# Attention in a two-layer trunk: the merge of the three patterns in half steps, the mask made first, v's splits and the affine rows in program order, two rows of o in v's buffer

## The chip, the core and the metric

The kernel runs on one core of a Trainium2 chip. The core has five engines with queues of their own: TensorE (PE in the profile, its weight loads PEld), VectorE (DVE), ScalarE (ACT), GpSimd (POOL) and SyncE (SP), which here issues the DMAs. Each engine takes its instructions in the order in which they were queued and waits, where needed, on semaphores. The metric is the device time of one execution in microseconds; lower is better.

## What is computed

The reference is a trunk of two layers over 1024 tokens of width 1024 in fp32. Layer 0 mixes tokens with a chunked gMLP, layer 1 with causal attention; a squared-ReLU MLP follows each. Each of the four sublayers is x <- LayerNorm(ALPHA * x + gate * f(h)), with h = x * (1 + scale) + shift, and shift, scale and gate from a conditioning vector. The part that the change touches is the attention, cut to its core:

```python
def dilated_branch(q, k, v, window, dilation, slopes):   # span = window // dilation = 128
    s = einsum('bnqrhe,bnkrhe->bnrhqk', qb, kb) * (E ** -0.5)   # kb: this block and the one before
    s = where(valid, s - slopes * dilation * diff, NEG)
    m = max(s); p = exp(s - m); l = sum(p)
    return einsum('bnrhqk,bnkrhe->bnqrhe', p / l, vb), m + log(l)

def mixer_b(h, w_qkv, w_out, slopes):
    qkv = (h @ w_qkv).reshape(B, S, N_PAT, 3, B_HEADS, B_HEAD_DIM)
    for g, (window, dilation) in enumerate(((128, 1), (512, 4), (2048, 16))):
        outs[g], lses[g] = dilated_branch(q_g, k_g, v_g, window, dilation, slopes)
    wts = softmax(lses over g)
    return sum_g(wts_g * outs_g) @ w_out
```

There are 16 heads of width 64, and every pattern g has q, k and v of its own.

## The kernel before

**Products in three passes.** TensorE multiplies pairs of fp32r numbers: a tensor is split into hi (a cast) and lo (what the cast lost), and a product is hi*hi + hi*lo + lo*hi. `split` (L100) makes the pair: the cast runs on ACT (L102), the subtraction on DVE (L103). Nearly every tensor goes through it, so these two lines stand for many tiles in the profile.

**Stages.** Mixer A, MLP 0, the values of all heads (`values`, L1123, which writes v to DRAM), attention (`attention`, L1252), its output projection (`OutRows`, L392), MLP 1. Memory for a stage is opened in pools when the stage is traced; a pool's tiles lie where those of the stage before lay, and each tile waits for the old tiles under it to be released. In `values` the pool at the lowest address holds the left forms S2 and S3, 16 KB of each partition apiece, of which S3 is used later; further up come the held weights, the x tiles and S4. In `attention` the pools are opened in the order `ql`, `vec`, `qk`, `qp` from the same address.

**Attention.** 24 groups, one for each of eight pairs of heads and each pattern in the order g = 2, 1, 0. A group takes eight slots, each with two half slots (`slots`, `at`, L1353 to 1358; here "+6.1" is the second half slot of the sixth slot after a group's first). Scores of a head's tile pairs, their softmax, the transposes of the probabilities (with a split into pThi and pTlo) and the products with v are hung into these slots; `project` (L1307), which computes q and k for the groups to come, is a generator that is advanced two matmul groups after each half slot. So TensorE always has projection matmuls between the steps of the softmax. A projection's PSUM bank, one of two, is released when its four pieces are split into q or k (L1340).

**v.** `load_v` (L1368) loads a group's v from DRAM into `v_raw`, of tag `raw` with two buffers, which the raw weights of q and k share, and splits it into `v`, of which there are two buffers.

**The mask.** `near` (L1270) holds distances, made by POOL with an iota and two selects; `far` is its right half, copied by DVE, with one corner filled. Both lie in `qp`. Each head's `bias` is a scaled copy.

**The merge.** After the three groups of a pair, `merge` (L1495) reads the softmax statistics, computes the weights of the patterns, writes them to DRAM and reads them back spread over the partitions (`bc`, 128x1024, three buffers of tag `res`). Then `scale(g)` multiplies each pattern's output by its weights, for g = 1 and 2 in a permuted order of elements, and `add` sums them; the sum goes to `o_dram`. These five steps on DVE stand in five half slots of the next pair's first group: +5.0, +5.1, +6.0, +6.1, +7.0.

**The affine rows.** `affine_row` (L1569): eight rows of the residual are loaded, multiplied and shifted by POOL and stored, for use after attention. They are hung into every second slot from +2.1 of the first group on, and use `res` buffers.

**The output projection.** `prepare(ch)` splits two rows of o at a time: rows 0 to 3 are loaded into `res` buffers, rows 4 to 6 into the `raw` buffers, the last row stays in SBUF. `out.load` loads the weights through `raw` too.

**The order of the work.** The program text gives a priority, not an order. A planner walks through the traced instructions with estimated durations, and at each point it queues on an engine the instruction that is ready by its estimates and comes first in the program. So an instruction whose inputs are early floats ahead of its place in the text. `tc.keep_in_program_order(ins)` ties an instruction behind the instruction traced just before it on the same engine; what is not tied may still float. The queues are fixed when the kernel is built.

## Time and profile before

| | |
|---|---|
| median of 3 runs | 2797.5 us (2794.14 to 2802.86) |
| profiled execution | 2792.79 us, of which the span from first to last instruction 2791.1 us |
| mean granted TensorE clock | 0.987 |
| busy: PE / DVE / ACT / POOL | 2697.5 / 2036.5 / 1424.1 / 189.2 us |
| attention, first score to last group's first score | 1267.0 to 2035.2 us |
| one pair of heads | 94.2 us (the first), 99.4 to 102.7 us (the next six) |

In a row of the timeline stand the start and the duration in us, the engine, the line, the operation, its tiles (out<-in), shapes and count, and in brackets how long the engine had been idle before it and what ended that. In a row of waits stand who waited, for what, the total in us, the number of times and the longest. In a row of a stretch stand its bounds and length, the busy time and number of instructions of each engine, the granted clock as a share of the full one, the DMA share and GB/s. A group's row has busy us and mean ns of one, then the engine's idle time just before.

### The profile page before, as it was taken

Reading aid. Unit: us, or ns where it says so; the run is one execution under the profiler, and the core shown is the slowest. Engines: PE = TensorE matmul, PEld = TensorE weight load, DVE = VectorE, ACT = ScalarE, POOL = GpSimd, SP = SyncE. Lnnn points to the kernel's source line nnn. Section 1 sums busy time; section 2 is a strip of 40 time slices with the busy share of each in tenths; the row PEclk is TensorE's granted clock in tenths of the full one; section 3 lists DMA queues with packets and bytes.
Section 4 is the critical chain, followed back from the end, with each engine's and each line's share of the span. In section 5 each row is a group of like instructions: output and inputs, shape, how many; then the busy total and the mean of one; then the engine's idle time right before and its main releaser. Section 6 shows DMA issues by size and latency. Waiting matters only on the chain.

```text
span 2791.1 us, 36348 instructions
## 1 busy us (share of the span) xinstructions
PE 2697.5 (97%) x12954; PEld 2244.4 (80%) x12954; DVE 2036.5 (73%) x3600; ACT 1424.1 (51%) x2639; POOL 189.2 (7%) x147
## 2 busy tenths in 40 slices
PE   6999999999999999989999999999998999999998
PEld 5787878887888888878888888888876788878887
DVE  6777797777967795445767767767679975668887
ACT  3354375555443553325665666666563755554332
POOL 1001000000000000043111111111020000000000
PEclk9999999999999999999999999999999999999999
DMA  7533347667845545353222213222234564486562
GB/s 257 166 121 107 120 158 226 219 223 273 295 142 191 165 144 158 121 187 101 62 62 78 74 51 85 77 55 78 85 89 154 171 209 154 158 284 210 171 200 90
DMA packets 317690, 416.63 MB, mean 149 GB/s; under 512 B 49164, under 2 KB 174516, under 8 KB 317508
## 3 DMA queue, kind: packets, MB, share of 16 engines
q1 hardware_dynamic: 317508, 414.31, 46.4%
q8 instruction: 101, 1.65, 0.3%
q14 instruction: 81, 0.66, 0.1%
HBM read 317.69 MB, written 96.55 MB: 148 GB/s over the span
## 4 chain that ended last, share of the span: by engine, by line
PE 73%; DVE 14%; DMA 7%; ACT 3%; issue 2%; POOL 1%; SPq 1%; POOLq 0%; DVEq 0%; ACTq 0%
PE psd L949 21%; PE psua L790 8%; PE psq L1332 8%; PE psk L1332 7%; PE psv L1237 7%; PE psuc L790 4%; PE psd_wout L367 3%; DMA adaw<-in_ada_w_dram 3%; PE pv L1459 2%; PE psu L367 2%; PE psd_wo L367 2%; PE psub L790 2%; PE psv L464 1%; DMA bc<-w_dram 1%; PE sc L1404 1%
## 5 line engine op out<-in xcount | busy, mean ns | idle before, releaser
L790 PE MATMUL psua<-right,left 128*128 128x512 f32 x1536 | 366.2, 392 | 3.3 <-ACT right L102 1.7
L949 PE MATMUL psd<-rhi,lhi 128*128 128x512 f32 x896 | 350.5, 391 | 3.0 <-ACT part L821 3.0
L949 PE MATMUL psd<-rlo,lhi 128*128 128x512 f32 x896 | 350.4, 391 | 0.2
L949 PE MATMUL psd<-rhi,llo 128*128 128x512 f32 x896 | 349.8, 390 | 0.0
L790 PEld LDWEIGHTS psua<-right,left 128*128 128x128 f32 x1536 | 288.1, 189 | 65.5 <-DVE right L103 2.9
L1413 ACT ACTIVATE p<-p,stat 128x128 f32<-128x128 f32 (+1 forms) x384 | 171.2, 446 | 147.2 <-DVE stat L1411 142.4
L949 PEld LDWEIGHTS psd<-rhi,lhi 128*128 128x128 f32 x896 | 168.9, 189 | 39.6 <-ACT part L821 3.9
L949 PEld LDWEIGHTS psd<-rlo,lhi 128*128 128x128 f32 x896 | 168.9, 188 | 36.1 <-DVE rlo L103 1.1
L949 PEld LDWEIGHTS psd<-rhi,llo 128*128 128x128 f32 x896 | 169.0, 189 | 35.1
L1332 PE MATMUL psk<-form_L,wk_hi 128*128 128x512 f32 x576 | 186.9, 406 | 9.7 <-DVE qlo L103 9.7
L790 PE MATMUL psuc<-right,left 128*128 128x512 f32 x768 | 187.8, 391 | 0.0
L1332 PE MATMUL psq<-form_L,wq_hi 128*128 128x512 f32 x576 | 184.9, 402 | 0.0
L103 DVE TENSOR_TENSOR pTlo<-pT,pThi 128x512 fp32r<-128x512 f32 (+1 forms) x160 | 99.6, 623 | 108.8 <-ACT pThi L102 108.5
L128 DVE SCALAR_TENSOR_TENSOR adaacc<-adaw,silu_c,adaacc 128x512 f32<-128x512 f32 x168 | 132.4, 799 | 56.0 <-DMA adaw<-in_ada_w_dram 55.1
L790 PEld LDWEIGHTS psuc<-right,left 128*128 128x128 f32 x768 | 143.4, 188 | 30.0 <-DVE right L103 0.5
L103 DVE TENSOR_TENSOR left<-ws,left 128x512 fp32r<-128x512 f32 x128 | 87.9, 688 | 73.0 <-ACT left L102 71.3
L103 DVE TENSOR_TENSOR llo<-lraw,lhi 128x1024 fp32r<-128x1024 f32 x112 | 136.3, 1217 | 0.8 <-ACT lhi L102 0.8
L102 ACT CAST left<-ws 128x512 fp32r<-128x512 f32 x128 | 79.3, 620 | 96.2 <-DVE ws L711 85.5
L1411 DVE CUSTOM_DVE_ANT_0 p<-sc,bias 128x128 f32<-128x128 f32 (+1 forms) x384 | 122.0, 346 | 8.7 <-PE sc L1405 6.2
L102 ACT CAST rhi<-rraw 128x1024 fp32r<-128x1024 f32 x48 | 50.6, 1054 | 142.9 <-issue 113.7
L1332 PEld LDWEIGHTS psk<-form_L,wk_hi 128*128 128x128 f32 x576 | 101.0, 191 | 25.2 <-issue 10.1
L1237 PE MATMUL psv<-vrhi,form_S 128*128 128x512 f32 x384 | 119.4, 389 | 0.2 <-DVE vpart L1214 0.2
(286 smaller groups left out, 6325.8 us busy)
## 6 DMA issues: line engine op xcount, KB each, us to landing
lraw<-forms SPq DMA_DIRECT2D x112, 512.0 KB
adaw<-in_ada_w_dram SPq DMA_DIRECT2D x192, 256.0 KB
up<-in_mlp_w_up_dram SPq DMA_DIRECT2D x64, 512.0 KB
forms<-s SPq DMA_DIRECT2D x128, 256.0 KB
rraw<-in_mlp_w_down_dram SPq DMA_DIRECT2D x64, 512.0 KB
forms<-part SPq DMA_DIRECT2D x96, 256.0 KB
vraw<-in_b_w_qkv_dram SPq DMA_DIRECT2D x26, 512.0 KB
spill<-acc SPq DMA_DIRECT2D x24, 512.0 KB
```

The source lines that it names most:

```text
L102: first = A.copy(hi, src) if hi_engine is A else hi_engine.tensor_copy(hi, src)
L103: return first, lo_engine.tensor_tensor(lo, src, hi, op=ALU.subtract)
L128: ins = V.scalar_tensor_tensor(acc[:], raw[:], silu_c[:, k : k + 1], acc[:], ALU.mult, ALU.add)
L367: T.matmul(dst, s[a], m[b], start=(n == 0), stop=(n == last))
L464: T.matmul(sums[u, half][:], units[u][a_][:, k * P : (k + 1) * P], hT[half][b_][:, k, :], start=k == 0 and a_ + b_ == 0, stop=k == KD - 1 ...
L790: T.matmul(acc, w[:, a, k, :], right[p][:, b, k, :], start=p in (1, 2, 5) and k + a + b == 0, stop=k == 3 and a == 1, skip_group_check=True)
L949: ins = T.matmul(sums[kind, m][:], l[a][:, k, m * P : (m + 1) * P], r[b][:, k, :], start=p in (1, 5, 2, 3) and kp + k + a + b == 0, stop=k ...
L1237: T.matmul(acc, left[:, a, 2 * kp + k, m * P : (m + 1) * P], r[b][:, k, :], start=p in (1, 2, 5) and kp + k + a + b == 0, stop=kp == 1 and ...
L1332: T.matmul(p[:], wu[a][:, k * P : (k + 1) * P], h_op(k, half, b), start=k + c_ == 0, stop=k == KD - 1 and c_ == 2)
L1411: V.tensor_tensor_reduce(out=pr[:, 0:w], in0=scb[:, sl], in1=st["bias"][:, width - w :], scale=-0.125, scalar=3e38, op0=ALU.add, op1=ALU.m ...
L1413: A.activation(pr[:, 0:w], pr[:, 0:w], AF.Exp, bias=nm, scale=-1.0, accum_out=l)
L1459: T.matmul(pvs[b][:, q0 % HALF : q0 % HALF + w_], stt, x_[:, o_ : o_ + w_], start=not begun[b], stop=left[b] == 0, skip_group_check=True)
```

## The change

It has five parts. `near` and `far` are made in the pool `ql`, ahead of the `qlo` tiles and their fills, which moves 1.5 KB of each partition from the last pool to the first. `load_v` moves from half slot +1 of slot base - 4 to half slot 0, and its split becomes a step of its own, `split_v`, in half slot +1 of slot base - 3, with both instructions tied in program order. `scale` and `add` work on one half of their tile at a time, ten steps in place of five; for the first seven pairs they stand in ten half slots, +6.0 to +10.1, for the last pair in the half slots of before, two each. The two POOL instructions of each affine row are tied in program order. Rows 4 and 5 of o are loaded by one DMA into one tile of v's tag, at the end of `output()`, in place of two `raw` tiles in `prepare(2)`.

```diff
-            near = qp.tile([P, 2 * P], F32, name="near", bufs=1)
+            near = ql.tile([P, 2 * P], F32, name="near")
...
-            far = qp.tile([P, P], F32, name="far", bufs=1)
+            far = ql.tile([P, P], F32, name="far")
             V.tensor_copy(far[:], near[:, P:])
             V.memset(far[64:P, 0:64], FAR)
+            qlo = [[ql.tile([P, S], F32R, name=f"qlo{e}_{b}") for b in range(2)] for e in range(2)]
...
-                @at(max(base - 4, 0), 1)
+                @at(max(base - 4, 0), 0)
                 def load_v():
-                    raw = wts.tile([P, NT, P], F32, name=f"v_raw_{hp}_{g}", tag="raw", bufs=2)
+                    my["raw"] = raw = wts.tile([P, NT, P], F32, name=f"v_raw_{hp}_{g}", tag="raw", bufs=2)
...
+                @at(max(base - 3, 0), 1)
+                def split_v():
+
                     my["v"] = vs = qp.tile([P, NT, 4, HEAD], F32R, name=f"v_{hp}_{g}", tag="v")
-                    split(vs[:, :, 0:4:3, :], vs[:, :, 1:3, :], raw[:].rearrange("p t (e c) -> p t e c", e=2))
+                    for x_ in split(vs[:, :, 0:4:3, :], vs[:, :, 1:3, :], my["raw"][:].rearrange("p t (e c) -> p t e c", e=2)):
+                        tc.keep_in_program_order(x_)
...
-                def scale(g):
+                def scale(g, half):
...
+                    n = o.shape[1] // 2
+                    o, bc = (t[:, half * n : (half + 1) * n] for t in (o, bc))
                     V.tensor_tensor(bc, o, bc, op=ALU.mult)
 
-                def add(g):
-                    V.tensor_tensor(box[0][:], box[0][:], box[g][:], op=ALU.add)
-                    if g == 2:
+                def add(g, half):
+                    w = slice(half * HALF, (half + 1) * HALF)
+                    V.tensor_tensor(box[0][:, w], box[0][:, w], box[g][:, w], op=ALU.add)
+                    if g == 2 and half:
...
-                for n, f in enumerate((lambda: scale(1), lambda: scale(2), lambda: scale(0), lambda: add(1), lambda: add(2))):
-                    at(base + 5 + n // 2, n % 2)(f)
+                steps = [lambda f=f, g=g, half=half: f(g, half) for f, g in ((scale, 1), (scale, 2), (scale, 0), (add, 1), (add, 2)) for half in range(2)]
+                for n, f in enumerate(steps):
+                    n = n + 12 if hp < N_PAIRS - 1 else n // 2 + 10
+                    at(base + n // 2, n % 2)(f)
...
-                G.tensor_tensor(t[:], t[:], affine["g"][:], op=ALU.mult)
-                G.tensor_tensor(t[:], t[:], affine["b"][:], op=ALU.add)
+                for n, op in (("g", ALU.mult), ("b", ALU.add)):
+                    tc.keep_in_program_order(G.tensor_tensor(t[:], t[:], affine[n][:], op=op))
...
+            def load_o(k):
+                if k == 4:
+                    both = qp.tile([P, 2, S], F32, name="oraw_4", tag="v")
+                    nc.sync.dma_start(both[:], o_dram[4:6].rearrange("k p t -> p k t"))
+                    box[5] = both[:, 1, :]
+                    return both[:, 0, :]
+                raw = row_bc(f"oraw_{k}") if k < 4 else wts.tile([P, S], F32, name=f"oraw_{k}", tag="raw", bufs=2)
+                nc.sync.dma_start(raw[:], o_dram[k])
+                return raw[:]
...
-                        raw = row_bc(f"oraw_{k}") if k < 4 else wts.tile([P, S], F32, name=f"oraw_{k}", tag="raw", bufs=2)
-                        nc.sync.dma_start(raw[:], o_dram[k])
+                        raw = box.pop(k, None) or load_o(k)
...
+                box[4] = load_o(4)
                 box["begin"] = out.begin()
```

More of the change, by code (lines that the diff above doesn't have):

```diff
@@ L1590, in prepare @@
                     if k == N_PAIRS - 1:
-                        raw = oTs["sum"]
+                        raw = oTs["sum"][:]
                     else:
-                        raw = row_bc(f"oraw_{k}") if k < 4 else wts.tile([P, S], F32, name=f"oraw_{k}", tag="raw", bufs=2)
-                        nc.sync.dma_start(raw[:], o_dram[k])
+                        raw = box.pop(k, None) or load_o(k)
                     for half in range(2):
```

7 lines of the change are left out of this document (3 added, 4 removed).

## The prediction

> **What bounds the kernel now.** I read the page first, then who waited for whom on TensorE in three stretches, then the stretches by engine, then the timelines of single engines around the long waits.
>
> ```profile
> span 2791.1 us, 36348 instructions
> PE 2697.5 (97%) x12954; PEld 2244.4 (80%) x12954; DVE 2036.5 (73%) x3600; ACT 1424.1 (51%) x2639; POOL 189.2 (7%) x147
> L103 DVE TENSOR_TENSOR left<-ws,left 128x512 fp32r<-128x512 f32 x128 | 87.9, 688 | 73.0 <-ACT left L102 71.3
> L103 DVE TENSOR_TENSOR llo<-lraw,lhi 128x1024 fp32r<-128x1024 f32 x112 | 136.3, 1217 | 0.8 <-ACT lhi L102 0.8
> ```
>
> TensorE is busy in 97% of the span, so only its own waits, and the slow clock behind them, can be won. The waits of 1200 to 1300, 1300 to 2000 and 2000 to 2200 us (total, times, longest) are:
>
> ```profile
> PE psk L1332 <- DVE qlo L103: 9.7, 1, 9.7
> ...
> PE pv L1459 <- DVE pTlo L103: 15.0, 6, 2.5
> ...
> PE psd_wo L367 <- DVE wo_lo L103: 2.4, 1, 2.4
> PE psd_wo L367 <- DVE acc L387: 2.3, 3, 1.0
> PE pv L1459 <- DVE pTlo L103: 2.3, 1, 2.3
> ...
> PE psd_wo L367 <- ACT wo_hi L102: 2.1, 1, 2.1
> ```
>
> So there is one wait of 9.7 us where attention begins, seven of about 2.5 us, one after each of the first seven pairs of heads, and some 7 us around the output projection. The stretches by engine (PE, PEld, DVE, ACT, POOL, then the granted clock) show what a merge costs: six pairs that hold one long wait each, one of these with a lowered clock, one without, and the first pair, which holds no merge.
>
> ```profile
> 1361.20:1967.20 606.00, 589.46 (x3333) 507.17 (x3332) 426.01 (x1074) 380.55 (x973) 69.96 (x72) 0.99 0.26 70
> 1361.20:1462.20 101.00, 98.51 (x558) 84.76 (x557) 71.02 (x179) 63.50 (x163) 11.71 (x12) 0.98 0.26 70
> 1564.90:1664.30 99.40, 96.90 (x557) 83.50 (x556) 70.92 (x179) 63.28 (x163) 11.71 (x12) 1.00 0.27 71
> 1267.00:1361.20 94.20, 94.20 (x535) 81.08 (x533) 59.57 (x156) 61.66 (x158) 24.55 (x18) 1.00 0.26 77
> ```
>
> The pair at full clock takes 99.40 us with 96.90 busy: 96.9 is a pair without a stall.
>
> **The change, part by part.**
>
> *The mask first, the affine rows pinned.* Attention's start on PE, ACT, POOL and DVE:
>
> ```profile
> 1236.88 0.61 PE L1332 MATMUL psq<-form_L,wq_hi 128*128 128x512 f32 x2
> ...
> 1237.56 0.61 PE L1332 MATMUL psq<-form_L,wq_hi 128*128 128x512 f32 x2
> ...
> 1248.10 1.19 PE L1332 MATMUL psk<-form_L,wk_hi 128*128 128x512 f32 x2 [9.70 <-DVE qlo L103]
> ...
> 1253.36 0.66 PE L1332 MATMUL psk<-form_L,wk_hi 128*128 128x512 f32 x2
> ...
> 1233.00 0.58 ACT L102 CAST q<-psq 64x512 fp32r<-64x512 f32 x1 [1.29 <-PE psq L1332]
> 1242.24 1.04 ACT L102 CAST v<-v_raw 128x1024 fp32r<-128x1024 f32 x1 [8.66 <-DMA v_raw<-v]
> ...
> 1241.35 2.35 POOL L1578 TENSOR_TENSOR aff<-aff,aff_b 128x1024 f32<-128x1024 f32 x1
> 1243.64 0.35 POOL L1271 IOTA near<- 128x256 f32 x1
> ...
> 1233.46 1.21 DVE L103 TENSOR_TENSOR wk_lo<-wk_raw,wk_hi 128x1024 fp32r<-128x1024 f32 x1
> 1244.97 0.23 DVE L1277 COPY far<-near 128x128 f32<-128x128 f32 x1 [10.30 <-POOL near L1274]
> 1245.11 0.68 DVE L103 TENSOR_TENSOR qlo<-psq,q 64x512 fp32r<-64x512 f32 x1
> ```
>
> The first projection's bank is released by two casts on ACT, each followed by a subtraction on DVE. The subtraction stands in DVE's queue behind the copy of `far`, which waits for `near`, which POOL makes behind an affine row. A second obstacle is in ACT's queue: the cast of v, waiting for its load, stands between the two casts of q. The change takes away both: the mask lies in the first pool, where S2 lay, and is traced first on POOL; the affine rows and v's split can no longer float ahead of what was traced before them. With both gone, cast, subtraction, cast, subtraction run from 1233.00, with wk_lo (to 1234.67) in between: 1234.67 + 0.68 + 0.58 + 0.68 = 1236.6. TensorE wants the bank after its last warm group, 1237.56 + 2 x 0.39, about 1238.4, so it does not wait. That wins 9.70 us, and the slow clock behind: four groups of three matmuls take 1253.36 - 1248.10 = 5.26 us where a warm group takes 1237.56 - 1236.88 = 0.68, four 2.72, so 2.5 more. Together 12.2 us. If only `far` got out of the way, the cast of v (to 1243.28) would be late next: 1243.28 + 0.58 + 0.68 = 1244.5, a gain of 3.6. I take 12.2, since the code moves both, and keep 3.6 as the lower end. `near` and `far` push the last `qlo` 1.5 KB into S3's place; its fill comes a pair's projections ahead of its use, so I take nothing.
>
> The pinned rows run inside the first pairs now. What a row of POOL does to DVE is seen earlier:
>
> ```profile
> 1205.36 2.39 POOL L1578 TENSOR_TENSOR aff<-aff,aff_b 128x1024 f32<-128x1024 f32 x1
> ...
> 1205.53 3.31 DVE L103 TENSOR_TENSOR vrlo<-v_r,vrhi 128x1024 fp32r<-128x1024 f32 x1 [1.76 <-ACT vrhi L102]
> ...
> 1209.36 1.21 DVE L103 TENSOR_TENSOR vrlo<-v_r,vrhi 128x1024 fp32r<-128x1024 f32 x1
> ```
>
> The same subtraction takes 3.31 us beside POOL and 1.21 alone: 2.1 us lost. In the first three groups stand nine such splits (wq, wk, v), so DVE loses at most 9 x 2.1 = 18.9 us, where it is busy 59.57 of 94.20. I take 0.5 us of TensorE's time, bounds 0 and 18.9. On SP the rows' loads and stores move back along with them, behind each other as before.
>
> *The merge in halves.* Around the fourth pair's merge DVE does this, and TensorE waits behind it:
>
> ```profile
> 1588.77 2.03 DVE L1543 TENSOR_TENSOR bc<-oT,bc 128x1024 f32<-128x1024 f32 x1 [1.02 <-DMA bc<-w_dram]
> 1591.10 2.00 DVE L1543 TENSOR_TENSOR bc<-oT,bc 128x1024 f32<-128x1024 f32 x1 [0.30 <-DMA bc<-w_dram]
> ...
> 1595.50 1.23 DVE L1543 TENSOR_TENSOR bc<-oT,bc 128x1024 f32<-128x1024 f32 x1
> ...
> 1596.97 1.22 DVE L1546 TENSOR_TENSOR bc<-bc,bc 128x1024 f32<-128x1024 f32 x1
> 1598.11 0.68 DVE L103 TENSOR_TENSOR pTlo<-pT,pThi 128x512 fp32r<-128x512 f32 x1
> 1598.71 1.22 DVE L1546 TENSOR_TENSOR bc<-bc,bc 128x1024 f32<-128x1024 f32 x1
> ...
> 1598.85 0.33 PE L1459 MATMUL pv<-pTlo,v 128*128 128x128 f32 x1 [2.50 <-DVE pTlo L103]
> ```
>
> Ahead of pTlo stand four whole steps, 2.03 + 2.00 + 1.23 + 1.22 = 6.48 us, and 1.32 us of waiting for the loads of `bc`. After the change the first half step stands in half slot +6.0, one slot later than now, so that the loads have landed. The pTlo in question belongs to half slot +6.1; two halves are traced before it, and a third may slip in. A half costs 0.688 us against 1.217 whole (the two rows of the page), so 0.16 more per split; the strided ones I estimate at half of 2.0 and 0.08, 1.08. Two or three halves are 2.2 to 3.2 us in place of 6.48 and 1.32: at least 4.6 less, more than the wait of 2.50. It should go.
>
> What is late next are the later packs of probabilities. Ten halves are 4 x 1.08 + 6 x 0.69 = 8.5 us, the five whole ones 7.7. They lie over five slots; eight slots are a third of 99.4, so five are 20.7 us. DVE without a merge is busy 59.57/94.20 = 63%, 13.1 us of these; with the halves 21.6, 0.9 more than there is. So DVE has no time to spare there, and each half that runs late delays a pTlo by up to a microsecond. I take 0.6 us per merge that remains, bounds 0 and the whole 2.5 with its clock.
>
> The seven merges cost now: six pairs 606.0 - 6 x 96.9 = 24.6 us, the seventh its wait of 2.3 and, as the mean of the others, 24.6/6 - 2.5 = 1.6 of slow clock, 3.9; together 28.5. Less 7 x 0.6 = 4.2 that leaves 24.3. The eighth merge keeps its slots; its steps are only cut in two, which lets TensorE's evictions (2.3 us of waits on `acc`) slip in between and costs 0.8 of DVE: nothing.
>
> A rule speaks to the clock part of that sum. The Trainium skill, "TensorE: Matmul & The Clock Gate", section "HAM oscillation", says that the clock falls with idle gaps above about 3.4 us. By it 2.5 us would never lower it, and the seven merges would be worth their waits alone, 15.0 + 2.3 = 17.3 us. The trace differs: 101.00 us at clock 0.98 and 99.40 at 1.00 hold one wait each of the same length (six make 15.0 us, the longest 2.5).
>
> *v's split.* Its load moves half a slot forward, its split to three slots ahead of its group and behind what was traced before it. Now:
>
> ```profile
> 1575.17 0.36 SPq L1373 DMA_DIRECT2D v_raw<-v  x1
> 1579.12 0.37 SPq L352 DMA_DIRECT2D wk_raw<-in_b_w_qkv_dram  x1
> ...
> 1610.00 1.05 ACT L102 CAST v<-v_raw 128x1024 fp32r<-128x1024 f32 x1
> ...
> 1600.26 1.22 DVE L103 TENSOR_TENSOR wk_lo<-wk_raw,wk_hi 128x1024 fp32r<-128x1024 f32 x1
> ```
>
> The load stands 35 us ahead of the split, so ACT doesn't meet an unlanded v. The raw buffer (one of two) stays taken some three slots, 12 us, longer; the loads of weights queued on SP behind it share the other. They stand far ahead too: 21 us for this wk. Nothing, with a loss where that lead is used up.
>
> *Rows of o in v's buffer.* One load of two rows in place of two, after the last but one v is released. SP is past its last projection weights there. Both splits can float, and their use is two partial products away. Nothing; the tail's waits of about 7 us (2.4 + 2.3 + 2.1) are the bound to the good, and to the bad one more such wait, of 2.4 us.
>
> **The sum.** 12.2 + 24.3 - 0.5 = 36.0. The profiled execution took 2792.8 us (span 2791.1 and 1.7 around it): 2756.8. The median of the runs, 2797.5, is 4.7 above; on that footing 2761.
>
> **The rivals.**
>
> *Half of the merge's stall stays* (DVE is full for five slots, and where the order is planned with shorter steps than the 2.0 us of the trace, pTlo comes late again): 12.2 + 14 - 0.5 gives 2772. For it speaks the sum of 21.6 in 20.7 us, against it that pTlo now follows two halves.
>
> *The start's wait passes on* to the cast of v or to another split: 3.6 in place of 12.2, 2770. Against it speaks v's pinned place behind the first scores.
>
> *The affine rows hold DVE up in the first pairs*, each of the nine splits in full: 18.9 on top, 2780. For it speaks the row of 3.31 us; against it the first pair's start, where POOL was as busy (24.55 us in that pair) and TensorE had 94.20 of 94.20. The Trainium skill, "GPSIMD Engine Reference", section "Key points", says that POOL shares its SBUF interfaces with VectorE, with contention where an instruction has two SBUF inputs; the trace agrees, 3.31 beside 1.21.
>
> *Slower: the raw buffers.* v holds one of two longer, projection weights arrive late, TensorE waits for a wq_lo or wk_lo. There are 48 projections; at 36.0/48 = 0.75 us each the gain is gone, and with 1 us each the time is 2809. For it speaks that SP and the buffers are taken in order; against it the lead of 21 us against 12 us of longer holding.
>
> *Nothing moves*: the queues come out as before, 2797.
>
> **How the numbers follow.** My case has 0.62, with 2751 to 2771; half the stall 0.14, the start's wait 0.06, the affine rows 0.05, the raw buffers 0.10, nothing 0.03. Faster by over 0.3% (8 us, about what a measurement of this kernel tells from no change) is 0.87, the same 0.03, slower 0.10. The low end takes the start, all seven merges and the tail: 2797.5 - 12.2 - 28.5 - 7 = 2750; the high end the start alone, 2785.
>
> **What would show it.** POOL makes `near` before 1210 us, DVE has no copy of `far` with a wait in front, and psk follows psq without a gap at full clock. Scores begin about 12 us earlier. Waits of pv on pTlo fall from 2.5 us to under 1 us each, and the pairs take 97 to 98 us at clock 1.00. DVE shows, for each pair, four half steps of about 1.1 us and six of 0.69. Wrong would be: a wait of psq or psk on wq_lo or wk_lo, pTlo still behind several halves, or ACT idle on v_raw.

## The result, and the profile after

The changed kernel takes 2815.7 us (median; 2810.3 to 2821.6) where the kernel before takes 2797.5 (2794.1 to 2802.9): the ratio is 1.0063, with an interval of 1.0040 to 1.0085. So it is 0.6% slower; 2761 had been forecast. The profiled execution of the changed kernel has a span of 2810.4 us, 19.3 more than before. One execution of the experiment e11 below took 8293 us where its other three took 2812 to 2815; its ratio leaves it out. The first two lines of the page of the changed kernel:

```profile
span 2810.4 us, 36355 instructions
PE 2702.6 (96%) x12954; PEld 2246.5 (80%) x12954; DVE 2037.3 (72%) x3640; ACT 1423.1 (51%) x2639; POOL 184.6 (7%) x147
```

The page hardly differs from the one before. The difference shows in the stretches by engine (length, then busy time of PE, PEld, DVE, ACT and POOL, granted clock, DMA). The first row goes from the first projection of the attention to its first score, the second covers the first pair of heads, the third the six pairs that follow, each with one merge in it:

```profile
1227.50:1254.70 27.20, 27.20 (x122) 22.52 (x120) 9.64 (x12) 6.76 (x10) 2.55 (x3) 1.00 0.23 68
1254.70:1373.80 119.10, 101.39 (x534) 85.02 (x533) 65.63 (x159) 63.94 (x161) 51.59 (x28) 0.91 0.37 112
1373.80:1987.10 613.30, 594.61 (x3332) 509.65 (x3331) 428.41 (x1104) 380.86 (x973) 65.08 (x72) 0.98 0.27 69
```

The same stretches of the kernel before, of which only the first was not shown yet:

```profile
1227.40:1267.00 39.60, 29.90 (x121) 24.22 (x120) 15.08 (x17) 10.94 (x14) 20.51 (x14) 0.87 0.63 200
```

The start became 39.6 - 27.2 = 12.4 us shorter, as forecast (12.2). The first pair became 119.1 - 94.2 = 24.9 us longer, and the six pairs 613.3 - 606.0 = 7.3 us longer in place of 21 shorter. What follows them is 0.6 shorter (823.9 before, 823.3 after). Together -12.4 + 24.9 + 7.3 - 0.6 = 19.2, the difference of the spans to a tenth. So two stretches carry the loss.

**The start.** From the timelines of POOL, DVE and PE:

```profile
1195.10 0.35 POOL L1266 IOTA near<- 128x256 f32 x1 [887.53 <-PE psv L1237]
...
1235.08 0.69 DVE L103 TENSOR_TENSOR qlo<-psq,q 64x512 fp32r<-64x512 f32 x1 [0.65 <-ACT q L102]
...
1237.70 0.61 PE L1332 MATMUL psq<-form_L,wq_hi 128*128 128x512 f32 x2
...
1238.38 0.61 PE L1332 MATMUL psk<-form_L,wk_hi 128*128 128x512 f32 x2
```

`near` is made at 1195, the bank's last subtraction ends at 1235.77, and psk follows psq 0.68 us later, without a gap and at full clock.

**The first pair.** TensorE now has one wait of 13.43 us there. Its chain, from the timelines of SP, ACT, DVE and PE:

```profile
1320.28 0.33 SPq L1588 DMA_DIRECT2D spill<-aff  x1
1322.91 0.32 SPq L1585 DMA_DIRECT2D aff<-spill  x1
1331.35 0.32 SPq L1588 DMA_DIRECT2D spill<-aff  x1
1333.93 0.32 SPq L1585 DMA_DIRECT2D aff<-spill  x1
1334.30 0.43 SPq L352 DMA_DIRECT2D wk_raw<-in_b_w_qkv_dram  x1
...
1338.79 1.04 ACT L102 CAST wk_hi<-wk_raw 128x1024 fp32r<-128x1024 f32 x1 [17.34 <-DMA wk_raw<-in_b_w_qkv_dram]
...
1316.66 1.34 DVE L103 TENSOR_TENSOR v<-v_raw,v 128x1024 fp32r<-128x1024 f32 x1 [0.39 <-ACT v L102]
...
1339.86 3.42 DVE L103 TENSOR_TENSOR wk_lo<-wk_raw,wk_hi 128x1024 fp32r<-128x1024 f32 x1 [18.03 <-ACT wk_hi L102]
...
1340.28 0.47 PE L1440 MATMUL pT<-ident,p 128*128 128x128 f32 x1 [13.43 <-ACT p L1417]
```

Read it backwards. TensorE waits for probabilities from ACT. ACT stands 17.34 us at the cast of a raw weight, with the exponentials queued behind it. The weight's load was issued only at 1334.30. v's subtraction, which frees a raw buffer, had ended at 1318.0; the load stands on SP behind stores and loads of affine rows. A row's store waits for POOL; the next load waits for that store, since the rows have one buffer; the next store waits for POOL again. The stores at 1320.28 and 1331.35 are 11.1 us apart, while the program asks for a row every two slots, some 8 us. So the rows fall behind, and what stands behind them on SP falls behind with them. The Trainium skill, "TensorE: Matmul & The Clock Gate", section "Architectural detail: the array is 16× 32×32, not 1× 128×128", says that ACT and DVE take their queues strictly in order; the idle 17.34 and 18.03 us agree.

**The six pairs.** The waits of TensorE in them (total, times, longest) have changed their name, not their size. Before it was 15.0 us on pTlo; after it is

```profile
PE pv L1463 <- ACT pThi L102: 13.2, 6, 2.4
PE pv L1463 <- DVE pTlo L103: 4.3, 6, 0.7
PE pT L1440 <- ACT p L1417: 1.1, 2, 0.6
```

The second merge, on DVE, with the wait on PE behind it:

```profile
1499.63 2.07 DVE L1549 TENSOR_TENSOR bc<-oT,bc 128x512 f32<-128x512 f32 x2 [2.38 <-DMA bc<-w_dram]
1501.62 0.28 DVE L1415 CUSTOM_DVE_ANT_0 p<-sc,bias 128x128 f32<-128x128 f32 x1
...
1502.04 1.03 DVE L1549 TENSOR_TENSOR bc<-oT,bc 128x512 f32<-128x512 f32 x1
1503.85 1.22 DVE L103 TENSOR_TENSOR v<-v_raw,v 128x1024 fp32r<-128x1024 f32 x1 [0.79 <-ACT v L102]
1505.10 0.69 DVE L103 TENSOR_TENSOR k<-psk,k 64x512 fp32r<-64x512 f32 x1
1505.82 1.09 DVE L1549 TENSOR_TENSOR bc<-oT,bc 128x512 f32<-128x512 f32 x1
...
1508.25 0.29 DVE L1415 CUSTOM_DVE_ANT_0 p<-sc,bias 128x128 f32<-128x128 f32 x1
...
1508.68 1.29 DVE L1549 TENSOR_TENSOR bc<-oT,bc 128x512 f32<-128x512 f32 x2
1509.88 0.68 DVE L1553 TENSOR_TENSOR bc<-bc,bc 128x512 f32<-128x512 f32 x1
1510.48 0.68 DVE L103 TENSOR_TENSOR pTlo<-pT,pThi 128x512 fp32r<-128x512 f32 x1
...
1510.18 0.33 PE L1463 MATMUL pv<-pThi,v 128*128 128x128 f32 x1 [2.36 <-ACT pThi L102]
```

Three things stand out. The first half steps wait 2.38 us for `bc`, and the scores of 1501.62 stand behind them; over the six pairs DVE stands 10.2 us in front of the scaled halves, as it did in front of the whole steps before (10.3). v's subtraction stands among the steps and waits 0.79 us for its cast. And seven half steps, not two or three, run ahead of pTlo: they floated forward. Which of the three counts, the trace alone doesn't say.

### The profile page after: what moved, and what is told of

The parts are those of the page before. It is cut to its first block, busy times and chain, and to the rows that moved or that the text cites. A ratio compares the mean times of both kernels' runs of the same rounds, so it can differ in the third digit from the quotient of the medians.

```text
span 2810.4 us, 36355 instructions
## 1 busy us (share of the span) xinstructions
PE 2702.6 (96%) x12954; PEld 2246.5 (80%) x12954; DVE 2037.3 (72%) x3640; ACT 1423.1 (51%) x2639; POOL 184.6 (7%) x147
## 4 chain that ended last, share of the span: by engine, by line
PE 72%; DVE 13%; DMA 8%; ACT 3%; issue 2%; POOL 1%; SPq 0%; POOLq 0%; DVEq 0%; ACTq 0%
PE psd L949 21%; PE psq L1332 8%; PE psv L1237 8%; PE psua L790 7%; PE psk L1332 6%; PE psuc L790 4%; DMA adaw<-in_ada_w_dram 3%; PE psd_wout L367 3%; PE pv L1463 2%; PE psu L367 2%; PE psd_wo L367 2%; PE psub L790 2%; PE psv L464 2%; DVE adaacc L128 1%; PE sc L1408 1%
## 5 line engine op out<-in xcount | busy, mean ns | idle before, releaser
L102 ACT CAST lhi<-lraw 128x1024 fp32r<-128x1024 f32 x112 | 117.3, 1048 | 4.1 <-PE psua L790 2.9
```

Of the source, the lines that this page charges most:

```text
L102: first = A.copy(hi, src) if hi_engine is A else hi_engine.tensor_copy(hi, src)
```

## The experiments

Each kernel is given by its stretches, taken in the same way as above: from the first projection to the first score ("start"), the first pair, the six pairs with a merge, and the rest to the end of the span, all in us; then the ratio to the kernel before on the same chip, with its interval.

| kernel | start | first pair | six pairs | rest | ratio |
|---|---|---|---|---|---|
| before | 39.6 | 94.2 | 606.0 | 823.9 | 1 |
| changed | 27.2 | 119.1 | 613.3 | 823.3 | 1.0063 (1.0040 to 1.0085) |
| e1: rows free | 35.3 | 108.6 | 613.0 | 822.8 | 1.0060 (1.0044 to 1.0075) |
| e2: rows at every third slot | 27.2 | 113.2 | 616.7 | 819.5 | 1.0064 (1.0040 to 1.0089) |
| e3: rows free, merge whole | 37.5 | 107.8 | 615.2 | 819.6 | 1.0039 (1.0019 to 1.0058) |
| e4: rows free, v as before | 39.5 | 94.2 | 602.4 | 819.8 | 0.9983 (0.9967 to 0.9998) |
| e5: rows pinned, v as before | 27.6 | 110.5 | 611.4 | 820.7 | 1.0008 (0.9993 to 1.0024) |
| e6: e5, first v pinned | 27.2 | 111.1 | 604.5 | 821.4 | 1.0020 (1.0004 to 1.0035) |
| e7: e6, halves pinned | 27.2 | 113.9 | 585.8 | 825.0 | 0.9947 (0.9928 to 0.9967) |
| e8: changed, rows on POOL's queue | 34.5 | 101.6 | 614.6 | 823.2 | 1.0034 (1.0020 to 1.0048) |
| e9: e7 without rows | 27.2 | 94.2 | 583.8 | 823.4 | 0.9888 (0.9874 to 0.9901) |
| e10: e4, halves pinned | 35.4 | 94.2 | 584.4 | 824.3 | 0.9916 (0.9903 to 0.9930) |
| e11: changed, halves pinned | 27.2 | 114.8 | 614.6 | 826.1 | 1.0068 (1.0050 to 1.0087) |
| e12: e7, rows in two buffers | 27.2 | 94.9 | 584.0 | 825.0 | 0.9887 (0.9871 to 0.9902) |
| e13: changed without rows | 27.2 | 98.0 | 614.2 | 822.2 | 1.0006 (0.9993 to 1.0020) |
| e14: e11, merge a slot later | 27.2 | 119.7 | 601.3 | 823.2 | 1.0039 (1.0026 to 1.0053) |

The work ahead of the attention differs by up to 10 us from profile to profile (the first projection comes between 1224 and 1234 us), so stretches are compared here, not spans. Each row comes from one profiled execution. Where two kernels do the same in a stretch, their figures show how far one can be trusted: e4 and e10 have the same start (39.5 and 35.4 us), e4, e5 and e6 the same merges and the same v in the six pairs (602.4, 611.4 and 604.5). Differences of that size in these two columns are not read below unless something else bears them out.

### Which pin, and which stretch

e1 undoes the pin of the affine rows.

```diff
-                for n, op in (("g", ALU.mult), ("b", ALU.add)):
-                    tc.keep_in_program_order(G.tensor_tensor(t[:], t[:], affine[n][:], op=op))
+                G.tensor_tensor(t[:], t[:], affine["g"][:], op=ALU.mult)
+                G.tensor_tensor(t[:], t[:], affine["b"][:], op=ALU.add)
```

> The changed kernel with one part undone: the two operations of an affine row are no longer pinned to their place on POOL. Theory A (SP's queue): in the changed kernel a row takes 12 us from load to store, rows are issued every two slots (8 us), so the rows fall behind, and loads of projection weights on SP stand behind stores and loads of rows that are not ready; TensorE's wait of 13.4 us at 1340 and most of the small waits of the first pair come from that. With the rows free they run from about 1205 us on again; the first pair falls from 119.1 to 94-97 us, the scores still begin at 1254-1256 (the start's gain is the mask's alone), the six pairs stay at 613 and the rest at 823: 2790-2795 on the footing of 2815.7. Theory B (v's pinned split holds up the first pair): the first pair stays above 110 us, 2808-2816. Theory C (the start's gain needed the pinned rows): scores begin at 1263-1267 again, about 2800.

Both halves of Theory A missed: the first pair stayed at 108.6 us, and the start lost 8.1 of its 12.4. The first score comes at 1264.5 us, as Theory C said, and the total of 2810.6 us lies in Theory B's range. Two rows from ACT's timeline of this run:

```profile
1247.55 1.05 ACT L102 CAST wq_hi<-wq_raw 128x1024 fp32r<-128x1024 f32 x1 [7.71 <-DMA wq_raw<-in_b_w_qkv_dram]
...
1285.42 1.05 ACT L102 CAST wk_hi<-wk_raw 128x1024 fp32r<-128x1024 f32 x1 [11.59 <-DMA wk_raw<-in_b_w_qkv_dram]
```

With the rows free again they run from 1205 us on, so that now a weight of the start is late behind them (7.71) and another one in the first pair (11.59). The rows' place moves the damage; the pair stays long.

e2 keeps the pin and issues the rows at every third slot.

```diff
-                at(2 + 2 * i, 1)(lambda i=i: affine_row(i))
+                at(2 + 3 * i, 1)(lambda i=i: affine_row(i))
```

> The changed kernel, rows pinned as in it, but issued at every third slot (12.3 us) in place of every second (8 us). Theory A (the rows fall behind because their chain of 12 us is longer than two slots, and SP's queue is then held up): the lag no longer grows, the wait of 13.4 us goes, the first pair takes 96-102 us: 2793-2799. Theory D (POOL's rows slow DVE's splits, 2.1 us each): the same eight rows still lie beside the same kind of splits, the first three groups take together with the next one nothing less: first pair 112-119 us, 2808-2816.

The wait of 13.4 us is gone (the longest is 3.3), but 113.2 us is only 5.9 less. The growing lag was part of it, and not the larger part. Both the pair and the total (2813.2 us) lie in the range of Theory D, that POOL's rows slow DVE's splits. Its mechanism is not borne out: in e12 below six of the eight rows run on POOL within the first pair, and it takes 94.9 us.

e3 undoes the rows' pin and the halves: `scale` and `add` are whole again, in the five half slots from +5.0.

```diff
-                steps = [lambda f=f, g=g, half=half: f(g, half) for f, g in (...) for half in range(2)]
-                for n, f in enumerate(steps):
-                    n = n + 12 if hp < N_PAIRS - 1 else n // 2 + 10
-                    at(base + n // 2, n % 2)(f)
+                for n, f in enumerate((lambda: scale(1), lambda: scale(2), lambda: scale(0), lambda: add(1), lambda: add(2))):
+                    at(base + 5 + n // 2, n % 2)(f)
```

> Rows free, and the merge's halves undone too: five whole steps, in the slots of the kernel before. v's split stays pinned half way through each group. Theory M1 (v's pinned split, 1.22 us and 0.8 us of waiting for its cast, now stands among the merge steps in front of the probabilities, and takes what the halves gave): the six pairs take 613-622 us, as much as with halves or more, and the total is 2790-2800. Theory M2 (the halves in their later slots are themselves what holds the probabilities up): the six pairs fall back to 606 or lower, total 2782-2788.

e4 undoes the rows' pin and v's.

```diff
-                @at(max(base - 4, 0), 0)
+                @at(max(base - 4, 0), 1)
                 def load_v():
...
-                @at(max(base - 3, 0), 1)
+                @at(max(base - 4, 0), 1)
                 def split_v():
...
-                    for x_ in split(...):
-                        tc.keep_in_program_order(x_)
+                    split(...)
```

> Rows free, and v's load and split as in the kernel before (one step, not pinned); the merge in halves stays. Theory M1 (v's pinned split is in the way of the merge): the six pairs fall from 613 to 588-600 us, the waits of pv on pThi and pTlo from 2.9 us together to under 1.7, total 2766-2780. Theory M2 (the halves are in the way): the six pairs stay at 610-615, total 2789-2795.

With whole steps and v pinned (e3) the six pairs take 615.2 us, as Theory M1 said (its total did not come: 2809.4 us, with a first pair of 107.8). With halves and v free (e4) 602.4, a little above what M1 expected. The waits of pv in e4 are 2.0 us for each merge, not under 1.7, and the total, 2790.1 us, lies where M2 had it; 12.3 us of that are the start's lost gain. What the order of the queues does shows best in TensorE's idle time, the length of a stretch less its busy time. In the six pairs it is 16.5 us before, 17.8 in e3, 12.6 to 13.3 with halves and v free (e4, e5, e6), and 18.4 to 19.1 with halves and v pinned (changed, e1, e2, e8, e13). So the halves by themselves save some 3 to 4 us of waiting, and v's pinned split adds some 6 and turns that into a loss. The rest of each difference is slower matmuls, and that part varies from execution to execution.

With neither pin the first pair is back at 94.2 us, and the start at 39.5: the mask first does not win the start by itself. Rows from DVE and ACT at the start of e4 show what is late in its place:

```profile
1218.85 0.23 DVE L1272 COPY far<-near 128x128 f32<-128x128 f32 x1 [1.98 <-POOL near L1269]
...
1241.72 0.58 ACT L102 CAST q<-psq 64x512 fp32r<-64x512 f32 x1
1252.21 1.05 ACT L102 CAST v<-v_raw 128x1024 fp32r<-128x1024 f32 x1 [9.91 <-DMA v_raw<-v]
1253.28 0.58 ACT L102 CAST q<-psq 64x512 fp32r<-64x512 f32 x1
```

`far` is copied 23 us ahead of the first cast of q, so the first obstacle is gone. The second holds: the cast of v stands between two casts of q and waits for its load, which SP issues behind stores and loads of rows.

The groups of v's subtraction show what the pin does to DVE, in the six pairs of the kernel before:

```profile
L103 DVE TENSOR_TENSOR v<-v_raw,v 128x1024 fp32r<-128x1024 f32 x18 | 22.0, 1221 | 0.1
```

and of the changed one:

```profile
L103 DVE TENSOR_TENSOR v<-v_raw,v 128x1024 fp32r<-128x1024 f32 x18 | 22.1, 1225 | 13.6 <-ACT v L102 13.6
```

The last column is the idle time of DVE in front of it. Pinned straight behind its cast, the subtraction waits 0.76 us on average; free, the planner gives it a place where the cast is done.

### The fourth corner, the order of the halves, the queue

e5 is the changed kernel with v's load and split as in e4 (the same edit); the rows stay pinned.

> The fourth corner: the affine rows pinned as in the changed kernel, v's load and split as in the kernel before; mask first, halves and rows of o as changed. So far the first pair took 94.2 us with neither pin, 108.6 with v's alone, 119.1 with both. Theory E (v's pinned split keeps one of two raw buffers until it is done, projection weights are then loaded late, and the rows' loads and stores ahead of them on SP make that worse; without v's pin the lead of the weights hides the rows): first pair 94-98 us. Theory F (the two pins hurt each by itself): 103-106 us. From the first projection to the first score: 39.6 us before, 27.2 changed, 35.3 with the rows free, 39.5 with neither pin; here v's cast may stand between the casts of q again, 28-36. Six pairs 602 as with v as before.

The first pair takes 110.5 us, far from Theory E and above the 103 to 106 of Theory F: the rows' pin by itself costs it 16.3 us. The waits of ACT on weights in it:

```profile
ACT wk_hi L102 <- DMA wk_raw<-in_b_w_qkv_dram: 13.0, 2, 8.1
```

The six pairs, expected at 602, came out at 611.4. The stretches of e4 and of e5 beside each other:

```profile
1367.80:1970.20 602.40, 589.79 (x3332) 505.70 (x3331) 427.87 (x1104) 379.76 (x973) 67.08 (x72) 0.99 0.27 70
1367.10:1978.50 611.40, 598.13 (x3333) 513.97 (x3332) 428.57 (x1105) 379.85 (x973) 66.93 (x72) 0.97 0.27 69
```

The idle time is nearly the same, 12.6 and 13.3 us; the busy time differs by 8.3, with a granted clock of 0.99 and 0.97. So 9 us between two kernels in this column can be the clock alone.

e6 adds the pin to the first group's v alone.

```diff
+                    for x_ in split(...):
+                        if n == 0:
+                            tc.keep_in_program_order(x_)
```

> As the run beside it (rows pinned, v as before), but v's split of the first group alone pinned, so that its cast doesn't stand between the casts of q. The start's gain needs both pins there: 27-28 us from the first projection to the first score. First pair under Theory E 94-98, under F 103-110; six pairs 602: total 2776-2783 under E (before, 2795 to 2797, less 12 at the start, 4 in the six pairs, 3 in the rest), 2786-2796 under F.

The start is as in the changed kernel, but e5 had 27.6 without this pin: that both pins are needed there was wrong, the rows' is enough. The first pair, 111.1 us, is just above Theory F's range, and the ratio of 1.0020 (2801.0 us, median) lies above the times that F gave. Against e4 and e10, which have neither pin, the rows' pin wins 8 to 12 us at the start and gives 17 back.

e7 pins the halves as well.

```diff
-                    V.tensor_tensor(bc, o, bc, op=ALU.mult)
+                    tc.keep_in_program_order(V.tensor_tensor(bc, o, bc, op=ALU.mult))
...
-                    V.tensor_tensor(box[0][:, w], box[0][:, w], box[g][:, w], op=ALU.add)
+                    tc.keep_in_program_order(V.tensor_tensor(box[0][:, w], box[0][:, w], box[g][:, w], op=ALU.add))
```

> As the kernel with v's first split alone pinned, and the merge's half steps pinned too, so that none can float ahead of what was traced before it. Theory G (what is left of the merge's wait, some 1.6 us and 2.6 of pair time, comes from halves that are moved forward, three and a half of them ahead of a pack's scores and three more ahead of its low part): the waits of pv on pThi and pTlo fall under 0.7 us, the six pairs from 602 to 583-592, total 10-18 us below the run without this pin. Theory H (DVE simply has no time left in those slots): the waits turn up some slots later, six pairs 598-606.

Theory G holds. The six pairs fall to 585.8 us, the median to 2781.8, 19 below e6 (10 to 18 were expected), and the view of TensorE's waits lists no more than this in them:

```profile
PE pT L1444 <- ACT p L1418: 2.5, 9, 0.4
PE pv L1464 <- DVE pTlo L103: 0.6, 1, 0.6
```

e8 is the changed kernel with the rows' loads and stores on POOL's queue.

```diff
-                nc.sync.dma_start(t[:], rows)
+                nc.gpsimd.dma_start(t[:], rows)
...
-                nc.sync.dma_start(rows, t[:])
+                nc.gpsimd.dma_start(rows, t[:])
```

> The changed kernel with both pins, but the loads and stores of the affine rows issued on POOL's queue in place of SP's, so that no weight stands behind a row. Theory A (SP's queue): the load of wk that came at 1334 is issued when its buffer comes free, about 1318; the wait of 13.4 us goes, the first pair falls from 119.1 to 96-108 us, total 2792-2804. If the raw buffers alone do it, the first pair stays at 112-119, total 2808-2816.

The waits of ACT for wk in the first pair, in the changed kernel:

```profile
ACT wk_hi L102 <- DMA wk_raw<-in_b_w_qkv_dram: 20.1, 3, 17.3
```

and with the rows on POOL's queue, beside the price at the start:

```profile
ACT wk_hi L102 <- DMA wk_raw<-in_b_w_qkv_dram: 0.6, 1, 0.6
...
1264.59 0.47 PE L1408 MATMUL sc<-k,q 128*128 128x128 f32 x1 [7.12 <-POOL q L1342]
```

SP's queue was the cause of the late weights: 20.1 us of waits became 0.6, and the first pair 17.5 us shorter. The rows also run earlier here, from 1201 us on; but in e1, where they run from 1205 us on and stand on SP, ACT waits 11.9 us for wk in the first pair, so it is the queue and not their time. But POOL now waits for its own DMAs with q's copies behind them, and TensorE's first score waits 7.12 us for one. That is why the total, 2806.0 us, came out above what was expected. The Trainium skill, "DMA: Bandwidth & Descriptors", section "Issuing engines are not separate DMA queues", says that DMAs from several engines save only the time of issuing, usually small. Here issuing is short too (0.32 to 0.43 us in the rows of SP above). What the second queue saves is the time that an issue stands behind others that wait for POOL or for a buffer, of which the page's sentence does not speak.

### The rows taken out, the best version, v against the merge

e9 is e7 without the affine rows.

```diff
-            for i in range(NT):
-                at(2 + 2 * i, 1)(lambda i=i: affine_row(i))
```

> The kernel with v's first split alone pinned and the merge's halves pinned, with the affine rows left out of the attention altogether (their scaling and shift of the kept residual is not computed, so the result lacks it). Theory A (rows on SP's queue and on POOL hold up the weights of the first pair): the first score comes 27.2 us after the first projection and the first pair takes 94-97 us in place of 114.0, waits of ACT on a raw weight vanish; total 2762-2766 where the kernel with rows has 2781.8. If the first pair stays above 105 us, the rows aren't the cause, and the order of the weight loads themselves is.

The start stays at 27.2 us and the first pair falls from 113.9 to 94.2: all that it lost there came from the rows.

e10 is e4 with the halves pinned as in e7.

> A version for the time: mask first, rows of o as changed, the halves pinned in program order, affine rows free and v as in the kernel before. First score 39.5 us after the first projection (no gain at the start), first pair 94.2, six pairs 584-588 as with the pinned halves, the rest 820-825: 2773-2779, below both kernels. If the halves' gain depends on the pins at the start, the six pairs stay at 600 and the time at 2788-2792.

It takes 2769.7 us (median), below what was expected. The six pairs are as expected; the start came out at 35.4 in place of 39.5. Its trace shows the second obstacle of e4 again, only shorter: `far` is copied at 1212.57 us, and the cast of v between the casts of q waits 7.23 us for its load, where it waited 9.91 in e4.

e11 is the changed kernel with nothing but the halves pinned.

> The changed kernel with both its pins, and the merge's half steps pinned as well: nothing else. Theory G (halves that float ahead of scores and low parts make the merge's wait, v's split only adds to it): the six pairs fall from 613.3 to 585-596, total 2788-2799; Theory M1 taken strictly (v's split at that place is enough for the wait): 604-613 and 2806-2816. The first pair stays near 119.

The six pairs stay at 614.6 us. With v pinned, an orderly merge at this place wins nothing: M1 taken strictly (604 to 613) is nearest. TensorE's idle time there is 24.5 us, against 3.1 in e7. DVE's idle time ahead of v's subtraction even rose:

```profile
L103 DVE TENSOR_TENSOR v<-v_raw,v 128x1024 fp32r<-128x1024 f32 x18 | 22.1, 1226 | 19.7 <-ACT v L102 19.7
```

e12 is e7 with the rows in two buffers in turn, loaded ahead and stored later.

```diff
+            def row_buffer(i):
+                if i % 2 == 0:
+                    return row_bc(f"aff_{i}")
+                return vec.tile([P, S], F32, name=f"aff_{i}", tag="oT", bufs=4)
...
+                at(2 + 2 * i, 1)(lambda i=i: row_load(i))
+                at(4 + 2 * i, 0)(lambda i=i: row_compute(i))
+                at(6 + 2 * i, 0)(lambda i=i: row_store(i))
```

> The kernel with v's first split and the halves pinned, where the rows take turns in two buffers (the usual one and the fourth buffer of the attention's sums, empty in the first pair), loaded two half steps ahead, stored two slots behind, so that a row's load need not wait for the store of the one before. Theory A: SP waits less on rows, the first pair falls from 114.0 to 97-106 us, total 2764-2775. If SP still waits at each store until POOL is done, 108-116, total 2776-2784.

The three stretches of this run:

```profile
1224.00:1251.20 27.20, 27.20 (x122) 22.52 (x121) 11.46 (x12) 6.77 (x10) 14.10 (x7) 1.00 0.39 126
1251.20:1346.10 94.90, 94.56 (x535) 81.08 (x534) 64.26 (x159) 64.28 (x161) 41.31 (x24) 1.00 0.41 123
1346.10:1930.10 584.00, 581.71 (x3332) 500.57 (x3331) 427.86 (x1105) 378.73 (x973) 69.16 (x72) 1.00 0.27 72
```

It takes 2761.9 us where the kernel before takes 2790.7 on the same chip, 28.9 less, and so beats both kernels and its own expectation. It takes as long as e9, which leaves the rows out. The edit gives the rows a second buffer and moves their loads, work and stores to new places; which of the two counts was not tried.

e13 is the changed kernel without the rows (the edit of e9).

> The changed kernel, v pinned as in it, with the affine rows left out of the attention (their scaling and shift of the kept residual is not computed, so the result lacks it). Theory A (in the first pair v's pin hurts only because SP reaches the late weight loads behind rows): first pair 94-98 us, first score 27.2 us after the first projection, total 2788-2795. Theory E (v's pinned split holds a raw buffer, which is enough to make the weights late): 100-108 us, total 2795-2805. The six pairs stay at 613-616 in both.

The first pair takes 98.0 us, at the upper edge of Theory A: v's pin alone costs it 3.8. TensorE waits 2.7 us there, all of it pv on pThi and pTlo; ACT waits 1.6 us for a raw weight in all, so late weights are not what these 3.8 are made of. With the rows on SP the same pin costs 14.4 where they are free (e1 against e4) and 8.6 where they are pinned (changed against e5).

e14 is e11 with the merge one slot later.

```diff
-                    n = n + 12 if hp < N_PAIRS - 1 else n // 2 + 10
+                    n = n + 14 if hp < N_PAIRS - 1 else n // 2 + 10
```

> The changed kernel with both pins and the merge's half steps pinned, and these begin one slot later, behind v's split. Theory I (in the run with both pins and pinned halves the first half step stood ahead of scores and waited 2.2 us for its load of bc, and that is what the six pairs lose): the wait is behind the scores now, the six pairs fall from 614.6 to 586-600, total 2787-2800. Theory J (v's subtraction, pinned straight behind its cast, makes DVE wait for ACT by itself): the wait of DVE for v's cast, 19.7 us in 18 splits of the six pairs there, stays above 12 us, and the six pairs stay at 606-615, total 2806-2815.

The idle time of DVE in front of the scaled halves and of v's subtraction:

```profile
L1549 DVE TENSOR_TENSOR bc<-oT,bc 128x512 f32<-128x512 f32 x36 | 33.7, 937 | 0.2
L103 DVE TENSOR_TENSOR v<-v_raw,v 128x1024 fp32r<-128x1024 f32 x18 | 22.1, 1226 | 19.8 <-ACT v L102 19.8
```

and in e7, where v is free but the merge no later:

```profile
L1550 DVE TENSOR_TENSOR bc<-oT,bc 128x512 f32<-128x512 f32 x36 | 34.2, 950 | 10.3 <-DMA bc<-w_dram 10.1
L103 DVE TENSOR_TENSOR v<-v_raw,v 128x1024 fp32r<-128x1024 f32 x18 | 21.9, 1218 | 0.0
```

Neither theory has it alone. A slot later the merge no longer waits for `bc`, and 614.6 - 601.3 = 13.3 us come back (8.9 of them idle time of TensorE). The other 601.3 - 585.8 = 15.5 us stay, with 19.8 us of waiting for v's cast. And e7 waits 10.3 us for `bc` without harm: in its queue the scores stand ahead of that wait. So a wait on DVE costs what stands behind it in the queue. How the 15.5 us divide between v's wait and its 1.2 us of work at that place was not tried.

## Why the prediction was wrong

**The start: the size was right, the reason in part.** 12.2 us were forecast, 12.4 came, and both obstacles were real. With the mask first and neither pin (e4, e10) the start takes 39.5 and 35.4 us, gains of 0.1 and 4.2, because the cast of v is late next: just the case for which the prediction kept 3.6 as the lower end. What it had wrong is what takes this second obstacle away. It counted on v's pin. With v's pin alone (e1) the start still takes 35.3 us, since another cast of ACT, of a wq, then waits 7.71 us for its load. With the rows' pin alone (e5) it takes 27.6 us, although the cast of v stands between the casts of q: SP issues the loads in time once the rows are out of its way. So the rows' pin, which the prediction counted for its work on POOL, won the start through SP. No run pins the rows and leaves the mask where it was, so what the mask adds to that stays open.

**The affine rows are the step that failed first.** It said "I take 0.5 us of TensorE's time, bounds 0 and 18.9" and priced the rows by what POOL does to DVE. That price is there: wk_lo at 1339.86 took 3.42 us beside a row, against 1.21 alone. But the sentence "On SP the rows' loads and stores move back along with them, behind each other as before" is where the loss lay. It counted the rows against each other, and not the weights behind them. Measured: 16.3 us for the rows' pin alone (e5 against e4), of which nothing is left with the rows out (e9) and 0.7 with them in two buffers (e12). The rows' rival, with 0.05, had the place and not the mechanism: it blamed POOL's hold on DVE, and e12 has most of that work in the first pair too.

**v's split was put at nothing, and failed twice.** In the first pair it adds 3.8 us without the rows, 8.6 with pinned rows and 14.4 with free ones. The slower rival had said that weights would be late; they were, but at a few places of the first pair, not by 0.75 us at each of 48 projections, and in the six pairs hardly any is late (ACT waits 1.2 us for wk there in all). Its reason, that v holds a raw buffer 12 us longer, is the wrong way round. In the first three splits of the six pairs v holds its buffer for 15 to 18 us from load to split, where it held it for 37 to 40 before. What became short is the lead of the next wk, whose load is issued when v's split has freed the buffer: its cast came 8.5 to 10.2 us after that load in the kernel before, and comes 3.6 to 4.9 us after it in the changed one. (The prediction's 21 us reach from the load to wk's subtraction; the cast came after 9.3.) That rows ahead of the load on SP therefore hurt sooner is likely, and was not tried by itself.

In the six pairs the step overlooked that a pin behind the cast makes DVE wait for ACT: 13.6 us in 18 splits, in the same slots as the merge. v's pin and its new place were changed together in every run, so which of them costs is not shown. Together they add 1.3 us to TensorE's idle time with whole steps (e3 against before), some 6 with free halves, and 24.5 - 3.1 = 21.4 with tied ones (e11 against e7). In time the last is 614.6 - 585.8 = 28.8 us; the other two are 9.2 and, on the means of e4 to e6 and of the five kernels with both, some 8, about what the clock alone made between e4 and e5.

**The merge: the size was right, the order wrong.** "two halves are traced before it, and a third may slip in" took the order of the text for the order of the queue. In the trace seven half steps stand ahead of pTlo, as an instruction that isn't tied may float. Nor had the loads of `bc` landed at +6.0, as the prediction had them: DVE stood 10.2 us in front of the scaled halves, and 10.3 with the halves tied there (e7); only a slot later is that wait gone (0.2, e14). With halves free and v as before the six pairs come out anywhere from 3.6 us shorter (e4) to 5.4 longer (e5). With the halves tied and v free (e7, e9, e10, e12) it is 20.2 to 22.2 us, where six of the seven merges were forecast to give 24.6 - 6 x 0.6 = 21.0. The forecast size came only with a tie that the change did not have. That DVE has "no time to spare" for five slots did not show: in e12 the waits of the six pairs are 584.0 - 581.7 = 2.3 us in all.

**The seventh merge and the tail** were forecast at 3.3 us and nothing; the rest of the span is 823.3 us in the changed kernel and 825.0 in e12, against 823.9. So nothing was won there. From the last pair's first score on, pv waited 4.5 us for pThi and pTlo before and 2.6 in the changed kernel, but the output projection (psd_wo) waited 6.8 us before and 11.9 after. So the tail, put at nothing, took back what the seventh merge gave; why these waits grew was not followed up.

## What to carry to other kernels

A pin doesn't only keep an instruction from running early; it puts every wait of that instruction in front of all that is queued behind it. Before pinning a step, list its DMAs and its inputs, and look at what follows it on each queue, the DMA-issuing one above all. A chain of load, compute and store through one buffer has a period (here 11 to 14 us from row to row in the changed kernel). Asked for more often, it holds its queue until the last row is done; here a second buffer with new places for the three steps took all but 0.7 us of that away. And where a planner may move steps, smaller steps alone need not help: they have to be tied to their places as well.

## What was not expected of the hardware

The clock. In the six pairs before, TensorE is busy 589.46 us in 3333 matmul records; in e12, with 3332, 581.71. Beside the 16.5 - 2.3 = 14.2 us of waiting the kernel before spends 7.8 us more on the same matmuls. All four kernels whose waits there are short (e7, e9, e10, e12; none above 0.6 us) are busy 581.7 to 582.7 us, at a clock of 1.00; the kernels whose longest waits there are 2.3 to 2.9 us are busy 589.5 to 598.1, at 0.97 to 0.99. So single waits of some 2.5 us lower the clock here, at a price that differs from execution to execution. The Trainium skill, "TensorE: Matmul & The Clock Gate", section "HAM oscillation", names idle gaps above about 3.4 us as what lowers the clock; no wait in these pairs is that long.
